# A two-layer decoder trunk on one core: the opening's loads and splits in order of need, MoBA's query projection ahead of the compression MLP, and ends of the attention's values behind the next softmax

## The chip, the cores and the metric

One core of a Trainium2 chip runs the whole program in one launch. The metric is the device time of one execution in microseconds (us), as the median of several runs. TensorE (PE) multiplies, VectorE (DVE) and ScalarE (ACT) do elementwise work, GpSimd (POOL) does a little of it, and SyncE (SP) issues most of the loads. Each engine runs its instructions in the order of the program, and waits on semaphores for the others.

## The reference

Two layers over 256 positions of width 1024, in float32: a SwiGLU block, a mixer of two attentions, a second SwiGLU block, and a norm at the end.

```python
for l in range(DEPTH):
    x = x + 0.5 * _swiglu(_rms(x, ffn1_norm[l]), ffn1_wg[l], ffn1_wu[l], ffn1_wd[l])
    h = _rms(x, mix_norm[l])
    (q_a, g_a, kc, vc, ks_, vs_, kw, vw, q_b, k_b, v_b, gate_a, gate_b) = _split_cols(h @ w_in[l])
    y_a = _nsa(q_a, g_a, kc, vc, ks_, vs_, kw, vw, ...) @ w_branch_nsa[l]
    y_b = _moba(q_b, k_b, v_b) @ w_branch_moba[l]
    merged = jax.nn.sigmoid(gate_a) * y_a + jax.nn.sigmoid(gate_b) * y_b
    x = x + merged @ w_out[l]
    x = x + 0.5 * _swiglu(_rms(x, ffn2_norm[l]), ffn2_wg[l], ffn2_wu[l], ffn2_wd[l])
return _rms(x, final_norm)
```

`_nsa` has 8 query heads in 2 groups. Besides window and selected attention it has a compressed branch: keys and values of 32 positions go through a small MLP (`gelu(flat @ w1) @ w2`), and the queries attend to 15 such summaries. `_moba` is, at this length, causal attention of 8 heads. Queries and keys of both are turned by rotary positions (rope).

## The kernel before, in words

**Numbers as two halves.** A float32 factor is written as `hi + lo`, two tensors that TensorE takes at its fast rate, and a product is three matmuls (`mm3`, lines 147 to 149: hi·hi, lo·hi, hi·lo). So each weight has to be split: ACT copies `raw` to `hi` (line 230, `split_hi`), DVE subtracts `hi` from `raw` to get `lo` (line 237, `split_lo`). Weights come in units of 128 x 2048 values (1 MB); three units of `raw` and four of `hi` and `lo` are held.

**The order of work.** The program is written from the view of TensorE. Each `mm3` is one *tick*. At a tick the program may put in a deferred step (`defer(n, f)`: n ticks later), the split of one more half unit (`split_tick`, every third tick at most), and a step of the *side* work, a generator that holds the attention (`attention`, `attend_all`) and gives TensorE a few transposes or small products every few ticks. So the long projections go on while the attention's chain of softmax and transposes runs through DVE and ACT. All of this is settled when the program is built; on the chip each engine follows its list.

**The mixer.** `ORDER` is the order in which the columns of `w_in` are projected: Q, KV2, G (which holds the keys for compression), QB (MoBA's queries), KB, VB, and four column blocks of the gates GA. `None` stands for `hidden`, the first layer of the compression MLP (`hh`, line 717), whose result ACT copies to `HH` (line 721). Each projection ends in a callback for each of the two row tiles. For queries that is `rope` (lines 528 to 536): three multiplies of DVE that read PSUM, an add, a copy by ACT to the hi half, and a subtraction by DVE for the lo half. The side work goes on with `compress` (`pK`, `X`), `keys_T` (`ksT`, lines 598 to 602), `queries_T` (`pQ`, `qT`, lines 587 and 588), `compress_more` (`hp`, `cp`, `kp`, lines 668 to 706), and then the attention itself: `s1` (scores `s`), `soft` (mask, maximum, exp to `P`), `s2_` (transposes `pt`), `s3` (values `o`), with `finish`, which scales the values on DVE (`aS`, line 616). Side transposes and the projections' PSUM tiles are in few banks: `tr`, `sc`, `a0`, `a1`. A transpose into `tr` waits until the readers of the tile two before have ended; `pQ` so waits for `ksT`'s subtractions on DVE.

**The opening.** `first_piece` computes the first product piece by piece, in eight slices of the first two units. `zeros` are matmuls of zeros that keep TensorE running ahead of it. `gain_columns` transposes the gains of a norm into columns (`pG`, `gcol`). x is transposed (`pT`), multiplied by the gains on DVE (`xg`), copied to hi by ACT and subtracted to lo by DVE (lines 347 to 352). `residual` adds a product to x and defers the transposes of the new x by `wait` ticks.

## Time and profile before

| | us |
|---|---|
| median of 3 runs (lowest, highest) | 1176.99 (1176.88, 1177.0) |
| the profiled execution | 1177.28 |
| its span in the trace | 1175.2 |
| TensorE busy | 1161.5 |
| DVE busy | 730.2 |
| ACT busy | 586.9 |
| POOL busy | 31.2 |

The granted TensorE clock was 0.998 of full speed. A row of the timeline gives start, duration, engine, line, operation, tiles (out<-in), how many instructions in a row it holds, and in brackets the idle time ahead of it with what ended it. A row of the waits gives who waited for whom, the sum, how many times, and the longest. Several instructions of one kind in a row stand in one line, and their duration is then from the first start to the last end. Engines overlap: a step may start while the one before it on the same engine ends, so durations add up to slightly more than the time that passes.

### The profile page before, as it was taken

To read this page: it belongs to the slowest core of one execution; us is meant where nothing else is said; L and a number is where in the kernel's file an instruction comes from. 1 tells how busy PE (TensorE), PEld (TensorE's weight loads), DVE (VectorE), ACT (ScalarE), POOL (GpSimd) and SP (SyncE) were. 2 spreads that over 40 slices of the span, in tenths; PEclk is the share of its full clock that TensorE was granted. 3 is DMA by queue.
4 is the path that set the end of the run, shared out by engine and by line. 5 is a ranking of instruction groups with operands and counts; after the bars stand their busy time and mean duration, and the time that the engine had idled before them with its cause. 6 is when DMAs were issued, how large, how long until landed. Compare 5 with 4: busy or idle time off the path is not lost.

```text
span 1175.2 us, 14436 instructions
## 1 busy us (share of the span) xinstructions
PE 1161.5 (99%) x5689; PEld 974.8 (83%) x5689; DVE 730.2 (62%) x1003; ACT 586.9 (50%) x929; POOL 31.2 (3%) x46
## 2 busy tenths in 40 slices
PE   8999999999999999999999999999999999999997
PEld 6888888988888888888888888889888888888886
DVE  6645546878857665545475455478787577645543
ACT  6444443567465464445364444346665644545332
POOL 2000000000100000000000000000001000000000
PEclk9999999999999999999999999999999999999999
DMA  8755462862444465555546555538434364665540
GB/s 278 258 194 179 144 243 93 208 193 94 143 143 145 143 236 193 185 174 214 180 154 204 187 188 199 174 117 217 144 109 144 117 204 125 238 208 164 180 179 36
DMA packets 103347, 203.53 MB, mean 173 GB/s; under 512 B 4560, under 2 KB 25504, under 8 KB 103280
## 3 DMA queue, kind: packets, MB, share of 16 engines
q1 hardware_dynamic: 102544, 201.84, 52.6%
q8 instruction: 45, 0.74, 0.3%
q10 hardware_dynamic: 432, 0.46, 0.1%
q0 software_dynamic: 304, 0.32, 0.1%
q14 instruction: 22, 0.18, 0.0%
HBM read 201.55 MB, written 1.05 MB: 172 GB/s over the span
## 4 chain that ended last, share of the span: by engine, by line
PE 90%; DVE 5%; ACT 3%; issue 1%; DMA 1%; SPq 0%; POOL 0%; POOLq 0%; DVEq 0%; ACTq 0%
PE pr L147 7%; PE pr L149 7%; PE pr L148 7%; PE dn L149 7%; PE dn L147 7%; PE dn L148 7%; PE u L147 6%; PE u L148 6%; PE u L149 6%; PE g L148 6%; PE g L147 6%; PE g L149 6%; PE pT L383 2%; DVE lo L237 2%; PE o L824 2%; PE gu L147 1%
## 5 line engine op out<-in xcount | busy, mean ns | idle before, releaser
L237 DVE TENSOR_TENSOR lo<-raw,hi 128x1024 fp32r<-128x1024 f32 (+3 forms) x386 | 457.0, 1214 | 209.0 <-ACT hi L230 208.7
L230 ACT CAST hi<-raw 128x1024 fp32r<-128x1024 f32 (+3 forms) x386 | 386.0, 1040 | 269.2 <-PE u L149 106.7
L147 PE MATMUL pr<-hi,hT 128*128 128x512 f32 (+2 forms) x320 | 126.0, 394 | 0.0
L147 PE MATMUL dn<-hi,aTh 128*128 128x512 f32 x318 | 124.6, 392 | 0.0
L147 PE MATMUL u<-hi,hT 128*128 128x512 f32 x320 | 124.6, 389 | 0.0
L149 PE MATMUL u<-hi,hT 128*128 128x512 f32 x320 | 124.5, 389 | 0.0
L148 PE MATMUL u<-lo,hT 128*128 128x512 f32 x320 | 124.5, 389 | 0.0
L149 PE MATMUL dn<-hi,aTl 128*128 128x512 f32 x318 | 123.8, 389 | 0.0
L148 PE MATMUL dn<-lo,aTh 128*128 128x512 f32 x318 | 123.7, 389 | 0.0
L147 PE MATMUL g<-hi,hT 128*128 128x512 f32 x312 | 123.6, 396 | 0.0
L148 PE MATMUL g<-lo,hT 128*128 128x512 f32 x312 | 121.7, 390 | 0.6 <-DVE lo L237 0.5
L149 PE MATMUL pr<-hi,hT 128*128 128x512 f32 (+2 forms) x320 | 122.0, 381 | 0.0
L148 PE MATMUL pr<-lo,hT 128*128 128x512 f32 (+2 forms) x320 | 121.7, 380 | 0.0
L149 PE MATMUL g<-hi,hT 128*128 128x512 f32 x312 | 121.7, 390 | 0.0
L385 DVE TENSOR_TENSOR aTl<-pT,aTh 128x512 fp32r<-128x512 f32 x40 | 25.8, 686 | 72.5 <-ACT aTh L384 72.5
L149 PEld LDWEIGHTS u<-hi,hT 128*128 128x128 f32 x320 | 60.1, 188 | 12.5
L147 PEld LDWEIGHTS u<-hi,hT 128*128 128x128 f32 x320 | 60.1, 188 | 12.5
L148 PEld LDWEIGHTS u<-lo,hT 128*128 128x128 f32 x320 | 60.1, 188 | 12.4
L149 PEld LDWEIGHTS dn<-hi,aTl 128*128 128x128 f32 x318 | 59.7, 188 | 12.4
L148 PEld LDWEIGHTS dn<-lo,aTh 128*128 128x128 f32 x318 | 59.7, 188 | 12.2
L147 PEld LDWEIGHTS dn<-hi,aTh 128*128 128x128 f32 x318 | 59.7, 188 | 12.0
L148 PEld LDWEIGHTS g<-lo,hT 128*128 128x128 f32 x312 | 58.7, 188 | 12.7 <-DVE lo L237 1.4
(221 smaller groups left out, 1584.8 us busy)
## 6 DMA issues: line engine op xcount, KB each, us to landing
raw<-in_ffn_wd SPq DMA_DIRECT2D x44, 1024.0 KB, 5.0
raw<-in_ffn_wu SPq DMA_DIRECT2D x40, 1024.0 KB, 5.1
raw<-in_ffn_wg SPq DMA_DIRECT2D x38, 1024.0 KB, 5.1
raw<-in_w_in SPq DMA_DIRECT2D x32, 1024.0 KB, 5.1
raw<-in_w_out SPq DMA_DIRECT2D x8, 1024.0 KB, 5.0
raw<-in_ffn_wg SPq DMA_DIRECT2D x10, 512.0 KB, 4.0
raw<-in_ffn_wu SPq DMA_DIRECT2D x8, 512.0 KB, 5.0
raw<-in_w_branch_nsa SPq DMA_DIRECT2D x4, 1024.0 KB, 5.1
```

The source lines that it names most:

```text
L147: nc.tensor.matmul(ps, x[0], w[0], start=start, stop=False)
L148: nc.tensor.matmul(ps, x[0], w[1], start=False, stop=False)
L149: nc.tensor.matmul(ps, x[1], w[0], start=False, stop=stop)
L230: nc.scalar.copy(done[i][0][:, a], raws[i][:, a])
L237: nc.vector.tensor_sub(lo[:, a], raws[i][:, a], hi[:, a].bitcast(F32))
L383: nc.tensor.transpose(p[:, k], src[:, 128 * k:128 * k + 128], ident)
L385: defer(1, lambda: nc.vector.tensor_sub(lo, p, hi.bitcast(F32)))
L824: nc.tensor.matmul(O["o"][:, i0 + i], st["pT"][:, i * nk + c], v(h, c, j), start=c == 0, stop=c == nk - 1)
```

## The change: what it does

1. `ORDER`: QB is projected before `hidden`, GA's first block after it. The weights are loaded and split in this order too.
2. `compress_more`: the transposed key `kp` and its split come ahead of the values' product `cp` with its mask `vbd`.
3. `attend_all`: `s3` hands back its end (`finish`, or POOL's sum of the compressed branch), and the end runs behind `soft` of the next pair.
4. `residual`: the ticks until the transposes. In the SwiGLU block, tile 0's second half goes from 4 to 8, tile 1's first half from 5 to 4; in the mixer the first halves go from 17 to 20 and 17.
5. The opening: the first loads are interleaved (x, weight slice, x, slices); the first gain row goes to ACT's queue; the other gains and constants go from POOL's queue to SP's at tick 24, with their columns at ticks 61 to 63; x is scaled straight from PSUM by ACT (hi) and DVE (lo) in slices of 128 columns; the first unit's `hi` is copied by DVE and two of its four `lo` are subtracted by POOL; products are put in as their slices come. The zeros are six and one, not five and three.

```diff
-ORDER = [C_Q, C_KV2, C_G, C_GA, None, C_GA + 512, C_QB, C_KB, C_VB, C_GA + 1024, C_GA + 1536]
+ORDER = [C_Q, C_KV2, C_G, C_QB, None, C_GA, C_GA + 512, C_KB, C_VB, C_GA + 1024, C_GA + 1536]
-WARM = (5, 3)
+WARM = (6, 1)
...
-    nc.sync.dma_start(graw[:, 0], gains[0])
     nc.scalar.dma_start(ident, T["ident"])
+    nc.scalar.dma_start(graw[:, 0], gains[0])
...
-    for what in ((0, 0), (1, 0), 0, 1, 2, 3, (0, 1), (1, 1)):
+    for what in ((0, 0), 0, (1, 0), 1, 2, 3, (0, 1), (1, 1)):
...
-    for j in range(1, len(NORMS)):
-        nc.gpsimd.dma_start(graw[:, j], gains[j])
-    for nm in CONSTS[1:]:
-        nc.gpsimd.dma_start(K[nm], T[nm])
...
+    def load_constants():
+
+        for j in range(1, len(NORMS)):
+            nc.sync.dma_start(graw[:, j], gains[j])
+        for nm in CONSTS[1:]:
+            nc.sync.dma_start(K[nm], T[nm])
...
-                    residual(nxt, t, h, ps[t][h], 4 + t)
+                    residual(nxt, t, h, ps[t][h], 8 if h > t else 4 + t * h)
...
+            yield None
+            kp = bank("tr", "kp", [128, G, 32])
+            nc.tensor.transpose(kp.rearrange("p g c -> p (g c)"), kc2.rearrange("p u d -> p (u d)"), ident[:64, :64])
+            nc.scalar.copy(kbd[:, :, 0], kp[:, :, 0:16])
+            nc.vector.tensor_sub(kbd[:, :, 1], kp[:, :, 0:16], kbd[:, :, 0].bitcast(F32))
             cp = bank("sc", "cp", [128, HD])
             nc.tensor.matmul(cp, hv.rearrange("p h c -> p (h c)"), w2[1], start=True, stop=True)
             vbd[0] = p2.tile([128, NH, HD], F32, name="vbd", tag="vbd", bufs=1)
             nc.vector.tensor_mul(vbd[0], cp[:, None, :].to_broadcast([128, NH, HD]),
                                  K["hmask"][:, :, None].to_broadcast([128, NH, HD]))
-            yield None
-            kp = bank("tr", "kp", [128, G, 32])
...
-                for j in pairs[i - 2]:
-                    j[3]()
+                ends = [j[3]() for j in pairs[i - 2]]
...
                 for j in pairs[i]:
                     j[1]()
+                for end in ends:
+                    if end is not None:
+                        end()
...
-                    lambda t, ps: residual(nxt, t, h, ps, 4 + t if h else 17))
+                    lambda t, ps: residual(nxt, t, h, ps, 4 + t if h else 20 - 3 * t))
...
+        def high(t, h, ks=range(4)):
+
+            for k in ks:
+                f = 4 * h + k
+                nc.scalar.activation(nrm.T[t][0][:, f], p[t][:, k], AF.Copy, scale=nrm.g[:, f:f + 1])
+
+        def low(t, h, ks=range(4)):
+            for k in ks:
+                f = 4 * h + k
+                nc.vector.scalar_tensor_tensor(nrm.T[t][1][:, f], p[t][:, k], nrm.g[:, f:f + 1],
+                                               nrm.T[t][0][:, f].bitcast(F32), op0=OP.mult, op1=OP.subtract)
+
+        def w_high(k):
+            nc.vector.tensor_copy(done[0][0][:, k], raws[0][:, k])
+
+        def w_low(q, k):
+            q.tensor_sub(done[0][1][:, k], raws[0][:, k], done[0][0][:, k].bitcast(F32))
...
-        defer(14 + j, lambda j=j: gain_columns(j))
-    defer(17, more_constants)
+        defer(60 + j, lambda j=j: gain_columns(j))
+    defer(24, load_constants)
+    defer(63, more_constants)
```

**DVE in the mixer.** DVE's list in layer 0 from the weight split ahead of `ksT` to the first small step of the MLP (`hy`), before. `lo<-raw,hi` is a weight's split, `ksT` the keys' second half.

```order
L237 TENSOR_TENSOR lo<-raw,hi 128x1024 x2
L602 TENSOR_TENSOR ksT<-pK_1876,ksT 128x512
L602 TENSOR_TENSOR ksT<-pK_1882,ksT 128x512
L237 TENSOR_TENSOR lo<-raw,hi 128x1024 x5
L674 TENSOR_TENSOR hy<-hx 128x30
```

The same stretch now, up to the last step of the second rope (`rt` and `qb` are QB's rope, one set for each row tile).

```order
L237 TENSOR_TENSOR lo<-raw,hi 128x1024
L531 SCALAR_TENSOR_TENSOR rt_1879<-pr,r,ropeq 128x512
L535 SCALAR_TENSOR_TENSOR rt_1881<-pr,r,ropeq 128x8x32 x2
L537 TENSOR_TENSOR rt_1879<-rt_1879,rt_1881 128x512
L539 TENSOR_TENSOR qb<-rt_1879,qb 128x8x64
L237 TENSOR_TENSOR lo<-raw,hi 128x1024
L605 TENSOR_TENSOR ksT<-pK_1898,ksT 128x512
L605 TENSOR_TENSOR ksT<-pK_1904,ksT 128x512
L237 TENSOR_TENSOR lo<-raw,hi 128x1024
L531 SCALAR_TENSOR_TENSOR rt_1946<-pr,r,ropeq 128x512
L535 SCALAR_TENSOR_TENSOR rt_1948<-pr,r,ropeq 128x8x32 x2
L537 TENSOR_TENSOR rt_1946<-rt_1946,rt_1948 128x512
```

One rope now stands between the two weight splits ahead of `ksT`, the other between `ksT` and the four splits that go ahead of `hy`.

**ACT in the mixer.** ACT's list from the copies of `ksT` to the MLP's `HH`, before. `gt` is the gates' tanh, `qT` NSA's transposed queries.

```order
L601 CAST ksT<-pK_1876 128x512
L601 CAST ksT<-pK_1882 128x512
L588 CAST qT<-pQ 128x512 x2
L920 ACTIVATE gt<-pr,rh 128x512
L230 CAST hi<-raw 128x1024
L588 CAST qT<-pQ 128x512 x2
L230 CAST hi<-raw 128x1024 x2
L721 COPY HH<-hh 128x256
```

And now, where the copies of the ropes (`qb`) stand in place of the tanh.

```order
L538 CAST qb<-rt_1879 128x8x64
L230 CAST hi<-raw 128x1024
L604 CAST ksT<-pK_1898 128x512
L604 CAST ksT<-pK_1904 128x512
L591 CAST qT<-pQ 128x512 x2
L538 CAST qb<-rt_1946 128x8x64
L230 CAST hi<-raw 128x1024
L591 CAST qT<-pQ 128x512 x2
L230 CAST hi<-raw 128x1024 x2
L724 COPY HH<-hh 128x256
```

ACT's second `qb`, which needs DVE's add, stands ahead of the second pair of `qT`, three weight copies and `HH`.

**DVE in the opening.** DVE's list up to the second unit's first split, before (`raw_87` is the first weight unit, `raw_96` the second; `hT_140` and `hT_149` the lo halves of x's two row tiles).

```order
L350 TENSOR_TENSOR xg_155<-pT_150,gcol_118 128x512
L352 TENSOR_TENSOR hT_140<-xg_146,hT_139 128x512
L352 TENSOR_TENSOR hT_149<-xg_155,hT_148 128x512
L237 TENSOR_TENSOR lo_162<-raw_87,hi_161 128x512 x4
L350 TENSOR_TENSOR xg_193<-pT_188,gcol_118 128x512
L350 TENSOR_TENSOR xg_200<-pT_195,gcol_118 128x512
L352 TENSOR_TENSOR hT_140<-xg_193,hT_139 128x512
L237 TENSOR_TENSOR lo_208<-raw_96,hi_207 128x1024
```

And now, from the third of the four copies that ACT did before (`hi_131<-raw_87`); the lo halves of x are `hT_134` and `hT_156`. Ahead of these rows stand two such copies and four steps of 128 columns for the first row tile.

```order
L1002 CAST hi_131<-raw_87 128x512
L998 SCALAR_TENSOR_TENSOR hT_156<-pT_157,gcol_110,hT_155 128x128 x2
L1002 CAST hi_131<-raw_87 128x512
L998 SCALAR_TENSOR_TENSOR hT_156<-pT_157,gcol_110,hT_155 128x128 x2
L1005 TENSOR_TENSOR lo_132<-raw_87,hi_131 128x512 x2
L998 SCALAR_TENSOR_TENSOR hT_134<-pT_181,gcol_110,hT_133 128x128 x4
L998 SCALAR_TENSOR_TENSOR hT_156<-pT_196,gcol_110,hT_155 128x128 x4
L237 TENSOR_TENSOR lo_207<-raw_96,hi_206 128x1024 x2
```

The steps on x of 512 columns, two for each half of a row tile, became sixteen of 128 columns, and the second unit's first split now comes behind all of them. ACT's table load, the first of its list after a transfer in before, stands behind a wait for the gain columns.

## Prediction

> **What bounds the kernel now.** I read the page first, then what TensorE (PE) waits for, then the timelines of the places that the change touches. On the page, the busy line and the chain that ended last:

> ```profile
> PE 1161.5 (99%) x5689; PEld 974.8 (83%) x5689; DVE 730.2 (62%) x1003; ACT 586.9 (50%) x929; POOL 31.2 (3%) x46
> ...
> PE 90%; DVE 5%; ACT 3%; issue 1%; DMA 1%; SPq 0%; POOL 0%; POOLq 0%; DVEq 0%; ACTq 0%
> ```

> TensorE is busy 1161.5 of 1175.2 us, and the change removes no matmul but one of the eight that only warm the engine up. So all that can be won is part of 13.7 us of idle time, and what can be lost is any wait that TensorE does not have yet. The waits of TensorE, longest sum first:

> ```profile
> PE pz L291 <- DVE zero L286: 1.5, 1, 1.5
> PE g L972 <- ACT hi L230: 1.4, 2, 1.2
> PE pt L815 <- ACT P L807: 1.3, 2, 0.7
> PE cp L698 <- issue: 1.2, 2, 0.6
> PE g L148 <- DVE lo L237: 0.5, 1, 0.5
> ```

> The first is the start itself. The second and the last lie in the opening; `pt` and `cp` come once in each of the two mixers. The change aims at these four, 4.4 us together. That is its ceiling, up to short gaps that this view leaves out.

> **The opening.** Four rows of before, from the timelines of ACT, DVE and PE:

> ```profile
> 1.19 1.28 ACT L351 ACT_TABLE_LOAD   x1 [1.19 <-PEq L1033]
> ```
> ```profile
> 4.21 0.17 DVE L304 COPY gcol<-pG 128x16 f32<-128x16 f32 x1 [2.81 <-PE pG L303]
> ...
> 14.67 1.22 DVE L237 TENSOR_TENSOR lo<-raw,hi 128x1024 fp32r<-128x1024 f32 x1 [0.26 <-ACT hi L230]
> ```
> ```profile
> 15.94 0.50 PE L148 MATMUL g<-lo,hT 128*128 128x512 f32 x1 [0.47 <-DVE lo L237]
> ```

> Earlier loads and smaller pieces let the first true product start sooner: the 1.4 us behind `hi` shrink, since a slice of raw weight is now copied as soon as it lands. But the opening is over only when the first product of the second weight unit has its `lo` (15.94 here, with DVE done at 15.89), and DVE decides that in the new order too. The table load is now behind the gain columns, so it starts near 4.4 + 0.3 (one more warming matmul ahead of them) and ends near 6.0, not at 2.47. The four scaled copies of x go there, then DVE's part. Prices for the small operations, from the same kinds on PSUM in the mixer (ACT's row first, then three that show DVE and the bank it frees):

> ```profile
> 215.40 0.36 ACT L902 ACTIVATE vv<-pr,r 128x128 f32<-128x128 f32 x1
> ```
> ```profile
> 216.05 0.35 DVE L528 SCALAR_TENSOR_TENSOR rt<-pr,r,c_rope 128x128 f32<-128x128 f32 x1
> 216.32 0.47 DVE L532 SCALAR_TENSOR_TENSOR rt<-pr,r,c_rope 128x64 f32<-128x64 f32 x2
> ```
> ```profile
> 217.16 0.34 PE L147 MATMUL pr<-hi,hT 128*128 128x408 f32 x1
> ```

> A 128-wide step costs DVE 0.27 (216.05 to 216.32), an ACT one about the same. From 6.0 four ACT copies take it to 7.1; then DVE has sixteen such steps (4.3), three of the four copies of raw weight and two subtractions of 512 columns, at about half of the 1.22 of the 1024-column row each (1.8 and 1.2), in all to 14.4 if it never idles. It does idle, for each next half of x has to be transposed and copied by ACT first: an estimate of 1.2 for three such hand-overs of about 0.4 (ACT's row and its semaphore). That is 15.6, and with the 1.22 of the first big `lo` 16.8, against 15.89: about 0.9 late. Two transposes of gain columns (moved to ticks 61 and 62) cost the same there. Less the warming matmul and the small gap that the earlier split of the next unit closes, I take +0.5. The lower bound is -1.4, the whole wait behind `hi`, if DVE never idles and the weight copies are quick. The upper is +2, below. No row shows a copy of fp32 from SBUF by DVE: bounds 0.2 and 0.69 each. [...]

> The nine constants' transfers go from POOL's queue to SP's, behind the first eight weight units and ahead of the next ones. At 0.4 to 0.5 of issue each they hold the next load by some 4 us; no row of the waits above names a DMA as TensorE's releaser, three raw units and four split ones stand ahead, and I cost it at nothing (bound +1).

> Two subtractions move to POOL. How the two engines get on, from the timelines of POOL and DVE at 305 us, and DVE alone at 244:

> ```profile
> 22.09 1.24 POOL L361 TENSOR_TENSOR r<-v,magic 128x1 f32<-128x1 f32 x2 [15.53 <-DVE v L357]
> ...
> 309.73 3.52 POOL L774 TENSOR_TENSOR A<-A,aC 128x512 f32<-128x512 f32 x2 [2.62 <-DVE aC L616]
> ```
> ```profile
> 244.61 3.50 DVE L237 TENSOR_TENSOR lo<-raw,hi 128x1024 fp32r<-128x1024 f32 x3 [0.69 <-ACT hi L230]
> ...
> 310.11 5.37 DVE L237 TENSOR_TENSOR lo<-raw,hi 128x1024 fp32r<-128x1024 f32 x3
> ```

> Three subtractions took 5.37 beside POOL and 3.50 without it: 1.9 for two POOL steps. In the opening most DVE steps read PSUM, so only a weight copy can meet a POOL step, once or twice: 0 to 1, taken at 0 within the +0.5. [...]

> **The mixer, MoBA's queries ahead of the MLP.** This is the term that decides. Before, DVE, ACT and PE ahead of and behind the hidden products:

> ```profile
> 234.39 2.35 DVE L237 TENSOR_TENSOR lo<-raw,hi 128x1024 fp32r<-128x1024 f32 x2
> 237.00 1.29 DVE L602 TENSOR_TENSOR ksT<-pK,ksT 128x512 fp32r<-128x512 f32 x2 [0.25 <-ACT ksT L601]
> ...
> 242.69 1.22 DVE L237 TENSOR_TENSOR lo<-raw,hi 128x1024 fp32r<-128x1024 f32 x1 [3.27 <-ACT hi L230]
> ```
> ```profile
> 240.05 1.08 ACT L588 CAST qT<-pQ 128x512 fp32r<-128x512 f32 x2 [2.60 <-PE pQ L587]
> ...
> 243.48 2.04 ACT L230 CAST hi<-raw 128x1024 fp32r<-128x1024 f32 x2
> 245.38 0.42 ACT L721 COPY HH<-hh 128x256 f32<-128x256 f32 x1
> ```
> ```profile
> 239.41 1.03 PE L587 MATMUL pQ<-c_ident,qa 128*128 128x128 f32 x8
> ...
> 245.85 0.41 PE L668 MATMUL hp<-c_sel,HH 128*128 128x32 f32 x2
> ...
> 250.60 0.33 PE L689 MATMUL cp<-w,hk 128*64 128x64 f32 x2
> ...
> 254.21 1.22 PE L796 MATMUL s<-ksT,qT 128*128 128x256 f32 x8
> ```

> What is put in there is the rope of QB, once per row tile, as it stands in before inside NSA's attention:

> ```profile
> 273.21 0.74 DVE L528 SCALAR_TENSOR_TENSOR rt<-pr,r,ropeq 128x512 f32<-128x512 f32 x1
> 273.88 0.86 DVE L532 SCALAR_TENSOR_TENSOR rt<-pr,r,ropeq 128x256 f32<-128x256 f32 x2
> ...
> 276.77 1.22 DVE L237 TENSOR_TENSOR lo<-raw,hi 128x1024 fp32r<-128x1024 f32 x1
> ```
> ```profile
> 275.50 0.62 ACT L535 CAST qb<-rt 128x512 fp32r<-128x512 f32 x1 [1.28 <-DVE rt L534]
> ```

> One rope holds DVE 3.56 (273.21 to 276.77), a handover to ACT in it; ACT's copy starts 2.29 after its first step. The new order puts the first between the two subtractions at 234.39, ahead of `ksT`. These `ksT` subtractions free the two banks that `pQ` needs, and pQ comes behind the same number of products as before. So `ksT` starts at 237.00 + 3.56 - 0.25 = 240.3, the first bank is free 0.65 later, at 240.95, and pQ starts 1.55 late. ksT's second ends at 241.6, one weight subtraction follows to 242.7, then the second rope; ACT's copy for it starts at 242.7 + 2.29 = 245.0. Behind it on ACT stand one weight copy (half of 2.04), two `qT` (1.08), two weight copies (2.04) and HH (0.42): 245.0 + 0.62 + 1.02 + 1.08 + 2.04 + 0.42 is 250.2, less some 0.1 of overlap at each of four joints 249.8. HH was done at 245.8, and `hp` on TensorE, which takes it, came right behind: 249.8 against 245.85, **3.9 late**. pQ's 1.55 and a wait for the first `lo` of the next unit lie within this.

> What could make it less: DVE's 3.27 of idle time at 239.4. But that idle comes behind `ksT`, and the rope is put ahead of it; it can only shorten what follows. Bounds: 2.4, if ACT is held by half of its queue alone, and 4.9, if the hand-overs cost more.

> **The key and value columns behind it.** `kp` is now ahead of the values' `cp`. DVE's end of kc and the value mask in before:

> ```profile
> 252.94 0.28 DVE L696 TENSOR_TENSOR kc<-ct,ct 64x128 f32<-64x128 f32 x1
> 253.15 0.68 DVE L700 TENSOR_TENSOR vbd<-cp,c_hmask 128x512 f32<-128x512 f32 x1
> ```

> kc is done 2.62 after cp (250.60 to 253.22), and `s` starts 3.61 after cp. The 0.6 wait of the second cp goes. But the mask now stands on DVE behind a weight subtraction (1.14) and the small step on kbd (0.1), and the scores' bank is free when it ends: 2.62 + 1.14 + 0.1 + 0.68 = 4.5, **0.9 later**, the cp wait already counted. Bounds -0.6 and +1.3; I take 0.8.

> **Ends behind the softmax, and no rope beside it.**

> ```profile
> 281.08 0.89 PE L815 MATMUL pt<-c_ident,P 128*128 128x128 f32 x4 [0.67 <-ACT P L807]
> ```

> DVE reaches this softmax late because the rope and the end of the values stand ahead of it. Both are gone from there, so the 0.67 goes with the shorter gap behind it: **-1.0** (bounds -0.6 and -1.2). The bank that an end frees comes up to two softmax steps later, and the next `o` is far enough behind: nothing, bound +0.5.

> **Later transposes.** The second half of row tile 0 is transposed eight ticks after its sum, not four. DVE then takes Q's rope later, and its margin at project G is 216.79 (216.32 + 0.47, bank freed) to 217.16. A multiply and a subtraction of 0.7 each that come late break it: 0 to 1.0, I take +0.4.

> **Sum.** Per layer 3.9 + 0.8 - 1.0 + 0.4 = +4.1, twice 8.2, opening 0.5: +8.7. The profiled execution took 1177.28, its span 1175.2 and 2.1 around it; the sum gives 1186.0 there. The median of the runs is 0.3 lower, so **1185.7**. With the bounds of its terms the case reaches from 1181 to 1190.

> **The rivals.**
> - *Slower, by POOL.* The first subtraction on POOL can start near 5.0 (gain columns at 4.4, one weight copy) and be done near 6.8, at half of 3.52. The product that needs it comes near 13: 15.94 less the wait of 0.47, one product and eight more at some 0.23 apart. If something holds POOL for longer than these 6 us, TensorE waits for the rest, and DVE's next two subtractions meet it as at 310.11: 1 to 2 above the forecast's opening, 1187. Against it: the first two POOL steps of before, at 22.09, took 1.24 together, with no gap. [...]
> - *No change.* pQ's 1.55 stays, and ACT has caught up by HH, so nothing of the rest: 1.55 + 0.2 - 1.0 - 0.6 per layer is about 0.2, with an opening of 0: 1177.3.
> - *Faster.* The rope costs nothing where it is put, since DVE's 3.27 and 0.69 of idle time (242.69, 244.61) hold both. Then the waits removed are all there is: per layer -1.0 - 0.6, twice, and -1.0 in the opening: 1172.8. It decides if pQ starts less than about 0.5 late. For it: 4 us of DVE idle before HH. Against it: the idle is behind `ksT`, and the two ropes take 7.1.

> **Chances.** Forecast 0.66, POOL 0.07, no change 0.10, faster 0.17. Slower 0.73, same 0.10, faster 0.17, where same is within 0.2%, or 2.4 us, about what a measurement of this kernel can tell from no change. The forecast's own range is 1181 to 1190. The range 1175 to 1189.5 adds the no-change case and leaves out most of the faster one and the top.

> **What would show it.** Right: TensorE's waits in both mixers name `pQ` on DVE (1.5 or so), `hp` on ACT's HH (over 1), `s` on DVE; `pt` and the second `cp` are gone; in the opening the first L148 starts near 16.9. Wrong: pQ within 0.5 of its product ahead, or HH's copy close behind `hh`. If the opening's L148 starts at 15 or earlier, DVE was quicker there than I count, and the opening term is a gain.

## The result, and the profile after

The changed kernel took 1190.93 us (median of four runs, 1187.64 to 1191.47) against 1176.99; the ratio is 1.0106, with a 95% interval of 1.0094 to 1.0119. So it is 12.5 us slower by the ratio and 13.9 by the medians. The direction and the cause in the mixers were forecast; the size, 8.7, was too small. The median lies 0.9 above the forecast's own range (1181 to 1190) and 1.4 above the other (1175 to 1189.5); the ratio times 1176.99 gives 1189.5, inside the first and at the edge of the second. The profiled execution took 1191.47, its span 1189.7, 14.5 more than before.

The busy times on the page of the changed kernel:

```profile
PE 1169.6 (98%) x5688; PEld 979.7 (82%) x5688; DVE 732.2 (62%) x1013; ACT 587.5 (49%) x937; POOL 34.3 (3%) x39
```

TensorE's busy time rose by 8.1 us, though it has one matmul fewer. That is the first thing to see: waits do not count as busy, so something made the matmuls themselves longer. The waits of TensorE in the changed kernel:

```profile
PE pQ L590 <- DVE ksT L605: 3.0, 2, 1.5
PE hp L671 <- ACT HH L724: 2.3, 2, 1.1
PE g L148 <- DVE lo L237: 1.8, 1, 1.8
...
PE pr L147 <- DVE rt L535: 1.2, 2, 0.6
PE pr L148 <- DVE lo L237: 1.2, 2, 0.6
...
PE s L801 <- DVE vbd L708: 0.5, 2, 0.3
```

`pt` and the second `cp` are gone, as forecast. Once in each layer there are now waits of `pQ`, of `hp`, of the first `lo` of GA, of `s`, and of the projection of G (`pr` for DVE's `rt`). The next table shows where the time went, by the start of the same product in both timelines. The last column is run e8 (below), in which TensorE is kept busy in its longest waits:

| place (TensorE) | before | after | late | late in e8 |
|---|---|---|---|---|
| first product of u, layer 0 | 22.32 | 26.57 | 4.25 | 0.40 |
| first product of dn | 135.75 | 140.63 | 4.88 | 1.02 |
| first `hh`, layer 0 | 240.21 | 247.88 | 7.67 | 3.82 |
| first `hp` | 245.85 | 255.51 | 9.66 | 5.81 |
| second `hp` | 248.24 | 259.47 | 11.23 | 5.80 |
| a product of the scores `s`, ahead of the old `pt` wait | 266.70 | 277.83 | 11.13 | 6.24 |
| one behind the old `pt` wait | 289.15 | 299.00 | 9.85 | 4.96 |
| just behind layer 0 (a product of u in layer 1's first block) | 605.51 | 615.23 | 9.72 | 4.91 |
| layer 1, second block (a product of dn) | 1108.49 | 1123.09 | 14.60 | 8.72 |

The mixer's chain in layer 0 of the changed kernel, as DVE, ACT and PE show it (rows that stand for those of before at 237.00, 245.38, 239.41 and 245.85):

```profile
244.38 0.69 DVE L539 TENSOR_TENSOR qb<-rt,qb 128x512 fp32r<-128x512 f32 x1 [0.69 <-ACT qb L538]
244.99 1.22 DVE L237 TENSOR_TENSOR lo<-raw,hi 128x1024 fp32r<-128x1024 f32 x1
246.13 1.28 DVE L605 TENSOR_TENSOR ksT<-pK,ksT 128x512 fp32r<-128x512 f32 x2
```
```profile
250.75 0.62 ACT L538 CAST qb<-rt 128x512 fp32r<-128x512 f32 x1 [2.00 <-DVE rt L537]
...
255.07 0.38 ACT L724 COPY HH<-hh 128x256 f32<-128x256 f32 x1
```
```profile
246.87 1.25 PE L590 MATMUL pQ<-c_ident,qa 128*128 128x128 f32 x8 [1.50 <-DVE ksT L605]
...
255.51 0.41 PE L671 MATMUL hp<-c_sel,HH 128*128 128x32 f32 x2 [1.14 <-ACT HH L724]
```

The rope and a weight split end at 246.2, then `ksT` frees the bank and pQ starts 1.5 after TensorE was ready; the second rope's copy on ACT starts at 250.75, and HH comes behind one weight copy, two `qT` and two more weight copies. HH is done at 255.45. Less the 5.8 by which TensorE is late ahead of `pQ`'s wait (4.9 from the opening, 0.9 at the projection of G) this is 249.7 in the times of before, where the forecast had 249.8.

What made the matmuls longer shows in the windows view. Its columns are the busy times of PE, PEld, DVE, ACT and POOL with the number of instructions, then PEclk (the granted TensorE clock as a share), the share of the DMA engines, and GB/s:

```profile
17.13:20.55 3.42, 1.57 (x7) 1.02 (x6) 3.27 (x6) 3.42 (x6) 0.00 (x0) 1.00 0.24 91
20.55:23.96 3.41, 3.41 (x10) 2.63 (x9) 2.84 (x7) 3.35 (x10) 0.54 (x1) 0.50 0.58 183
```
```profile
245.83:249.24 3.41, 2.37 (x19) 2.20 (x20) 3.41 (x6) 1.61 (x3) 0.00 (x0) 1.00 0.02 5
...
252.65:256.06 3.41, 1.68 (x8) 0.89 (x7) 2.72 (x3) 3.41 (x6) 0.00 (x0) 1.00 0.06 22
256.06:259.48 3.42, 3.42 (x10) 2.63 (x9) 2.55 (x7) 1.57 (x4) 0.00 (x0) 0.50 0.84 281
```

The granted clock is cut in steps of 3.41 us that all lie on one grid. Behind a step in which TensorE was busy for 1.57 or 1.68 of 3.41, the next runs at half speed (a *fall* of the clock, below); behind one of 2.37 it does not. The clock falls at 20.55, at 256.06 and at 839.74 in layer 1, which is 2, 71 and 242 steps behind its first full speed at 13.72, and each time behind the waits that the change brought. In such a step matmuls of 512 columns come every 0.43 and not every 0.23, and about 1.6 us are lost: between the two `hp` of the table the changed kernel falls back by 1.57, where e8 does not. Before, the clock did not fall between 6.2 us and 1170. The emptiest step there was the first:

```profile
6.23:9.64 3.41, 2.03 (x8) 1.08 (x8) 1.52 (x3) 2.50 (x5) 0.34 (x4) 1.00 1.03 362
```

The clock has a second part in the opening. TensorE's first products before, and in the changed kernel below them:

```profile
8.10 0.51 PE L972 MATMUL g<-hi,hT 128*128 128x512 f32 x1 [1.17 <-ACT hi L230]
8.82 2.79 PE L972 MATMUL g<-hi,hT 128*128 128x512 f32 x11 [0.21 <-ACT hi L230]
```

```profile
6.82 0.80 PE L976 MATMUL g<-hi,hT 128*128 128x512 f32 x1 [0.54 <-ACT hT L993]
...
9.28 4.19 PE L976 MATMUL g<-hi,hT 128*128 128x512 f32 x9
...
19.59 0.50 PE L148 MATMUL g<-lo,hT 128*128 128x512 f32 x1 [1.85 <-DVE lo L237]
```

The first product does start earlier, at 6.82 against 8.10. But nine products take 4.19 us where eleven took 2.79 before, since TensorE did not come to full speed until 13.7 (6.2 before); up to then its products come every 0.43. The transposes behind them, and with them DVE's part, move along, and the first `lo` product is at 19.59, not 15.94 as before or near 16.9 as forecast. In e8, where TensorE is at full speed from 6.7, it is at 17.37.

### The profile page after: what moved, and what is told of

It is laid out like the page before. It is cut to its first block, busy times and chain, and to the rows that moved or that the text cites. A ratio compares the mean times of both kernels' runs of the same rounds, so it can differ in the third digit from the quotient of the medians.

```text
span 1189.7 us, 14437 instructions
## 1 busy us (share of the span) xinstructions
PE 1169.6 (98%) x5688; PEld 979.7 (82%) x5688; DVE 732.2 (62%) x1013; ACT 587.5 (49%) x937; POOL 34.3 (3%) x39
## 4 chain that ended last, share of the span: by engine, by line
PE 89%; DVE 6%; ACT 3%; issue 1%; DMA 1%; POOL 0%; SPq 0%; POOLq 0%; ACTq 0%; DVEq 0%
PE dn L149 7%; PE dn L148 7%; PE dn L147 7%; PE pr L147 6%; PE pr L149 6%; PE pr L148 6%; PE u L147 6%; PE u L148 6%; PE u L149 6%; PE g L149 6%; PE g L148 6%; PE g L147 6%; PE o L829 3%; PE pT L386 2%; DVE lo L237 2%; PE s L801 2%
## 5 line engine op out<-in xcount | busy, mean ns | idle before, releaser
L237 DVE TENSOR_TENSOR lo<-raw,hi 128x1024 fp32r<-128x1024 f32 (+1 forms) x382 | 455.6, 1223 | 201.9 <-ACT hi L230 201.4
L230 ACT CAST hi<-raw 128x1024 fp32r<-128x1024 f32 (+1 forms) x382 | 383.1, 1044 | 272.2 <-PE u L149 110.4
L147 PE MATMUL pr<-hi,hT 128*128 128x512 f32 (+2 forms) x320 | 127.3, 398 | 1.2 <-DVE rt L535 1.2
L147 PE MATMUL u<-hi,hT 128*128 128x512 f32 x320 | 124.7, 390 | 0.0
L148 PE MATMUL u<-lo,hT 128*128 128x512 f32 x320 | 124.5, 389 | 0.0
L148 PE MATMUL pr<-lo,hT 128*128 128x512 f32 (+2 forms) x320 | 123.2, 385 | 1.2 <-DVE lo L237 1.2
L147 PE MATMUL dn<-hi,aTh 128*128 128x512 f32 x318 | 124.4, 391 | 0.0
L147 PE MATMUL g<-hi,hT 128*128 128x512 f32 x312 | 124.0, 398 | 0.0
L148 PE MATMUL g<-lo,hT 128*128 128x512 f32 x312 | 122.1, 391 | 1.8 <-DVE lo L237 1.8
L148 PE MATMUL dn<-lo,aTh 128*128 128x512 f32 x318 | 123.7, 389 | 0.0
L149 PE MATMUL pr<-hi,hT 128*128 128x512 f32 (+2 forms) x320 | 123.4, 386 | 0.0
L148 PEld LDWEIGHTS g<-lo,hT 128*128 128x128 f32 x312 | 59.1, 189 | 13.9 <-DVE lo L237 2.3
L149 PEld LDWEIGHTS u<-hi,hT 128*128 128x128 f32 x320 | 60.1, 188 | 12.5
L147 PEld LDWEIGHTS u<-hi,hT 128*128 128x128 f32 x320 | 60.1, 188 | 12.5
L148 PEld LDWEIGHTS u<-lo,hT 128*128 128x128 f32 x320 | 60.1, 188 | 12.4
L147 PEld LDWEIGHTS pr<-hi,hT 128*128 128x128 f32 x320 | 60.7, 190 | 11.5 <-ACT hi L230 1.8
L148 PEld LDWEIGHTS pr<-lo,hT 128*128 128x128 f32 x320 | 60.8, 190 | 11.1 <-DVE lo L237 1.8
```

Of the source, the lines that this page charges most:

```text
L147: nc.tensor.matmul(ps, x[0], w[0], start=start, stop=False)
L148: nc.tensor.matmul(ps, x[0], w[1], start=False, stop=False)
L149: nc.tensor.matmul(ps, x[1], w[0], start=False, stop=stop)
L230: nc.scalar.copy(done[i][0][:, a], raws[i][:, a])
L237: nc.vector.tensor_sub(lo[:, a], raws[i][:, a], hi[:, a].bitcast(F32))
```

## The experiments

Two theories were tried. **The forecast's:** the engines' lists are worked in order, and the ropes put ahead of `ksT` and HH make TensorE wait. **The clock:** on top of that, waits that fill about half a step of 3.41 us cost another 1.6 us behind them, and in the opening they delay full speed. The rivals: that the order of the projections is not what costs, that the waits are all there is, or that a bank is the cause. Times are medians; the ratio and its interval are to runs of the kernel before on the same chip. The runs were made on three chips: e1 to e4, e5 to e8, and e9 to e12.

| run | median us | ratio to before (95%) |
|---|---|---|
| the changed kernel | 1190.93 | 1.0106 (1.0094 to 1.0119) |
| e1 order only | 1183.32 | 1.0045 (1.0033 to 1.0058) |
| e2 old order | 1178.81 | 1.0011 (1.0002 to 1.0019) |
| e3 old opening | 1187.60 | 1.0080 (1.0066 to 1.0094) |
| e4 ends only | 1174.95 | 0.9980 (0.9971 to 0.9989) |
| e5 fill in the opening | 1187.61 | 1.0083 (1.0069 to 1.0097) |
| e6 zeros in the first gaps | 1186.77 | 1.0079 (1.0065 to 1.0093) |
| e7 fill in the mixers | 1185.63 | 1.0080 (1.0066 to 1.0094) |
| e8 all three fills | 1185.82 | 1.0069 (1.0056 to 1.0082) |
| e9 ends, and zeros in the first gaps | 1174.77 | 0.9973 (0.9964 to 0.9983) |
| e10 residual only | 1179.49 | 1.0013 (1.0004 to 1.0022) |
| e11 kp only | 1177.26 | 0.9999 (0.9990 to 1.0008) |
| e12 keys in another bank | 1190.18 | 1.0099 (1.0084 to 1.0115) |

### e1: the new ORDER alone

```diff
-ORDER = [C_Q, C_KV2, C_G, C_GA, None, C_GA + 512, C_QB, C_KB, C_VB, C_GA + 1024, C_GA + 1536]
+ORDER = [C_Q, C_KV2, C_G, C_QB, None, C_GA, C_GA + 512, C_KB, C_VB, C_GA + 1024, C_GA + 1536]
```

> The kernel before with the new ORDER alone. Theory (in-order lists, and a TensorE clock that falls to half for 3.4 us behind a stretch with about 2 us of idle time): pQ waits 1.5 on DVE, hp 1.1 to 1.4 on ACT's HH, the first lo 0.6, in both layers, the pt wait of 0.7 goes, the second cp wait stays; and the granted clock falls once in each mixer, for 1.6 to 1.7. Per layer 3.9 - 1.2 + 1.6, twice: about 1185.5. Rival A (the waits without the clock): 1182.4. Rival B (the order of the projections is not what costs, but the opening): within 2 of before.

Its waits, and the steps of its grid that hold the waits ahead of `hp` in layer 0 and part of those in layer 1:

```profile
PE pQ L587 <- DVE ksT L602: 3.0, 2, 1.5
PE hp L668 <- ACT HH L721: 2.3, 2, 1.1
```
```profile
246.38:249.79 3.41, 1.69 (x10) 0.94 (x8) 2.53 (x3) 3.41 (x7) 0.00 (x0) 1.00 0.28 105
```
```profile
819.82:823.23 3.41, 1.99 (x9) 1.31 (x7) 2.72 (x5) 2.54 (x4) 0.00 (x0) 1.00 0.75 278
```

The waits are those of the changed kernel to the tenth. In layer 0 `hp` is 3.87 late (my sum: 3.9). The clock fell there, behind the step with 1.69 busy; it did not fall in layer 1, where the same waits lie across the joints of the grid and the emptiest step had 1.99. So layer 0 ends 3.5 late and layer 1 adds 2.5. The five times lie at 1183.4 with a clock of 0.997 and at 1182.4 with 0.999. Both theories are half met: the waits alone are rival A's 1182.4, and the clock adds 1 on some executions only, less than I gave it.

The `pt` wait is gone in this run too, as expected, though the end of the values still stands ahead of the softmax. The row that waited 0.67 before starts without a wait, and the products behind it win back 1.3 in each layer:

```profile
285.07 0.61 PE L815 MATMUL pt<-c_ident,P 128*128 128x128 f32 x4
```

### e2: the changed kernel with the old ORDER

```diff
-ORDER = [C_Q, C_KV2, C_G, C_QB, None, C_GA, C_GA + 512, C_KB, C_VB, C_GA + 1024, C_GA + 1536]
+ORDER = [C_Q, C_KV2, C_G, C_GA, None, C_GA + 512, C_QB, C_KB, C_VB, C_GA + 1024, C_GA + 1536]
```

> The changed kernel with the old ORDER. Theory: no pQ, hp or lo waits in the mixers and no fall of the clock there; what stays is the opening (4.9 late after the gain columns) and the later transposes (0.9 per layer), less the pt waits that the ends behind the softmax take away (1.0 each): about 1181. Rival B (the opening holds nearly all): 1188 or more.

```profile
PE g L148 <- DVE lo L237: 1.8, 1, 1.8
...
PE s L801 <- DVE vbd L708: 1.3, 2, 0.7
PE pr L147 <- DVE rt L535: 1.1, 2, 0.6
```

It is 1178.81, 12 below the changed kernel and 0.1% above before: rival B falls, the order is what costs most. In its profiled execution the opening is 4.88 late, as in the changed kernel, and each mixer then adds 0.9 at project G and 0.4 at the scores and gives 1.3 back: nothing. That execution took 1181.57; the eleven lie between 1177.76 and 1181.57, which is 0 to 4 above the median of before on this chip. Since the mixers come out even, I put this down to the opening; only one of the eleven was profiled.

### e3: the changed kernel with the opening of before

The loads, zeros, splits and constants of before, with ORDER, `residual`, `compress_more` and `attend_all` of the changed kernel.

> The changed kernel with the opening of before (loads, splits, zeros, constants), all mixer changes kept. Theory: the opening costs 4 to 5 in the changed kernel, so 1186 to 1187, with the mixer waits as in the changed kernel and two falls of the clock. Rival (the opening costs the 0.5 of the forecast, and the rest of the 13.9 is in the mixers): 1190.

1187.60, with the waits in both mixers, but a fall of the clock in layer 1 alone (835.22) and not in both. It is some 3 below the changed kernel, by the medians or the ratios, whose intervals just touch. That is the opening's share, less than the 4 to 5 expected. In this profile the opening of before was itself 1.68 late at the first u, with a fall at 9.19.

### e4: the ends behind the softmax, alone

```diff
-                for j in pairs[i - 2]:
-                    j[3]()
+                ends = [j[3]() for j in pairs[i - 2]]
...
+                for end in ends:
+                    if end is not None:
+                        end()
```

> The kernel before with the ends of the values behind the softmax alone (attend_all and s3). Theory: the softmax on DVE comes 1.3 earlier, which takes the pt wait away in both layers though the rope is still there: 1.0 to 1.2 per layer, 1174.6 to 1175.0. Rival (the rope alone holds the softmax up, and the ends only move the wait to the next values): 1177.

DVE's timeline, where the softmax steps (L804, L806) now stand ahead of the end (`cf`, `aS`):

```profile
279.31 1.22 DVE L237 TENSOR_TENSOR lo<-raw,hi 128x1024 fp32r<-128x1024 f32 x1
280.45 0.42 DVE L804 TENSOR_TENSOR s<-s,c_causal 128x256 f32<-128x256 f32 x1
280.91 0.69 DVE L806 TENSOR_REDUCE m<-s 128x2 f32<-128x512 f32 x1
```

The `pt` wait is in none of its waits, and the same products lie 1.28 earlier in layer 0 and 1.33 in layer 1, with the rope still in its place. So moving the end is enough, and the rival falls. But moving the rope is enough too (e1), for the same 1.3 per layer. They are two ways to win one wait, and not two gains: the new ORDER takes the wait away also without the ends. Alone, without the new ORDER, this part of the change is worth 0.2%.

### e5 to e8: useless matmuls in the waits

e5 adds seven zeros ahead of the first mm3, e6 more zeros in the first gaps, e7 matmuls into a bank of their own ahead of pQ (seven) and hp (five), e8 all of it. Every part of the computation stays.

```diff
+        zeros(7)                          # e5, at the end of first_piece
-WARM = (6, 1)
+WARM = (6, 3)                             # e6
+        zeros(3)                          # e6, between the first two products
+            idle(7)                       # e7, ahead of queries_T(qa, qaT)
+                if j == 0:
+                    idle(5)               # e7, ahead of the first hp
...
+        def idle(n):
+            pz = bank("sc", "pi", [128, 512])
+            h = nrm.T[0][0]
+            for i in range(n):
+                nc.tensor.matmul(pz, h[:, 0], h[:, 0:4].rearrange("p a b -> p (a b)"), start=i == 0, stop=i == n - 1)
```

> The changed kernel with seven useless matmuls of zeros more at the end of first_piece, where TensorE waits 1.85 for the first lo of the second unit; they leave out nothing. Theory of the clock: the zeros take 1.6 of that wait, the stretch counts as busy, and the fall to half behind it (20.5 to 24.0) goes: 1.7 faster than the changed kernel, 1189.2. Rival (the clock does not look at idle time, or the slow stretch has another cause): the same time or up to 0.3 more, since seven matmuls are added.

> The changed kernel with five zeros more in the first gaps: (6, 3) instead of (6, 1), and three between the first two products. Theory of the clock: full speed comes near 7 to 10 and not at 13.7, which saves up to 13 of the 19 slow products at 0.2 each, 2 to 2.7, of which the later wait for lo (DVE sets it, from the transposes that TensorE does) takes back a part: 1 to 2.5 faster than the changed kernel, 1188.4 to 1189.9. Rival (DVE's chain alone sets the end of the opening): the same time.

> The changed kernel with useless matmuls in both mixers: seven of 512 columns ahead of pQ, five ahead of the first hp, into a bank of their own. Theory of the clock: the waits for DVE and ACT stay as long, but TensorE is busy in them, and the falls of the clock (256.1 and 839.7) go: 3.2 faster than the changed kernel, 1187.7, with 24 matmuls more. Rival (waits alone): the same time or more.

> The three fillings together. Theory: the gains add up to what the waits alone cost, 1183 to 1185, with a granted clock of 1 from about 10 us to the end. Rival: 1190.

The steps that were too empty are fuller now, in e5 (the first `lo`) and in e7 (ahead of `hp`):

```profile
18.26:21.67 3.41, 3.34 (x15) 2.77 (x16) 3.41 (x5) 3.38 (x8) 0.00 (x0) 1.00 0.27 54
```
```profile
252.34:255.76 3.42, 2.83 (x14) 1.88 (x14) 2.73 (x3) 3.42 (x6) 0.00 (x0) 1.00 0.17 64
```

All four are faster than the changed kernel though they have more matmuls: by 3.3, 4.2, 5.3 and 5.1 at the medians. They may have run on another chip than it did; by the ratios to before it is 0.23, 0.27, 0.26 and 0.37%, where the intervals of e5 and e7 reach that of the changed kernel's (1.0094), e6's ends just below it and e8's (up to 1.0082) lies clear of it. A fill takes away the falls where it is, and no others: e5's profile still falls at 253.78 in layer 0, and e6's at 18.68 and in both mixers. In e7's profile no step in a mixer is slow, and in e8's none at all from 6.7 to 1180.9, 2.9 us ahead of the end (mean clock 0.999). What the rival has in its favour is only that e7's profiled execution, whose opening stays slow, took 1189.35. By the medians the first three won more than expected (1.7, up to 2.5, and 3.2), and e8 less: it stayed above its 1183 to 1185. In e5 it was not the added zeros alone: ahead of them its profile was at full speed from 4.6 to 8.0 and again from 11.4, and that of the changed kernel only from 13.7. So the fills do not add up by their medians: e8 is no faster than e7, whose five times lie at 1185.6 or at 1189.3. But e8's own five lie within 0.3, and the others' within 1 to 3.8. In e6 and e7 the times go with the mean clock (e7: 1189.3 at 0.997, 1185.6 at 0.998 and 0.999; e6: 1189.22 at 0.994, 1187.63 at 0.995, 1186.6 to 1186.8 at 0.996); in e5 they do not (1186.75 and 1187.53 at 0.996, 1187.69 and 1187.73 at 0.998).

The waits that are left in e8:

```profile
PE s L809 <- DVE vbd L710: 1.3, 2, 0.7
PE pr L148 <- DVE lo L237: 1.2, 2, 0.6
PE pr L147 <- DVE rt L535: 1.2, 2, 0.6
```

e8 is thus the changed kernel without the falls of the clock: it is 8.7 late near the end, and the sum of the forecast was 8.7. Its last column in the table above splits this as opening 1.0 and 3.9 and 3.8 for the mixers.

### e9: the ends, and zeros in the first gaps of before

```diff
-WARM = (5, 3)
+WARM = (5, 5)
-        some(0, 0, 0, (0, 1))
+        some(0, 0, 0, (0,))
+        zeros(1)
+        some(0, 0, 0, (1,))
```

with e4's edit.

> The kernel before with the ends behind the softmax, and three zeros more in the opening's first gaps: (5, 5) for (5, 3), and one between the first two products. Theory: the ends give 1.3 per layer, and the zeros keep the first gap from counting as idle, so that the clock falls in the opening in no execution: 1174.7 with a spread under 1. Rival (the spread of before, 1176.6 to 1179.7, has another cause than where the clock's stretches lie): the same median as with the ends alone and the same spread of 3.

PE's first products here, and in e4 below it:

```profile
6.10 2.08 PE L291 MATMUL pz<-zero 128*128 128x512 f32 x5
8.29 0.50 PE L973 MATMUL g<-hi,hT 128*128 128x512 f32 x1
8.63 0.39 PE L291 MATMUL pz<-zero 128*128 128x512 f32 x1
8.86 2.81 PE L973 MATMUL g<-hi,hT 128*128 128x512 f32 x11
```
```profile
8.15 0.50 PE L973 MATMUL g<-hi,hT 128*128 128x512 f32 x1 [1.13 <-ACT hi L230]
10.36 4.14 PE L973 MATMUL g<-hi,hT 128*128 128x512 f32 x11 [1.70 <-ACT hi L230]
```

This beats both kernels: 1174.77, 0.27% below before, and nine times within 0.8 (1174.30 to 1175.06), where those of before on the same chip spread over 3.3, and e4's eleven, on another chip, over 3.1. By the ratios e9 and e4 cannot be told apart. In e4's profile the second wait for `hi` was 1.70, the step behind it ran at half speed, and eleven products took 4.14, not 2.81. The zeros closed the gap here. In e4's profile ACT also had to wait longer for the second slice of raw weight; how much of the scatter is the loads and how much the clock, these runs do not part.

### e10, e11: residual's ticks alone, kp ahead of cp alone

```diff
-                    residual(nxt, t, h, ps[t][h], 4 + t)
+                    residual(nxt, t, h, ps[t][h], 8 if h > t else 4 + t * h)
-                    lambda t, ps: residual(nxt, t, h, ps, 4 + t if h else 17))
+                    lambda t, ps: residual(nxt, t, h, ps, 4 + t if h else 20 - 3 * t))
```

> The kernel before with the new waits of residual alone. Theory: one wait of 0.6 (0.9 by start times) at project G in each layer, nothing else: 1.9 slower, 1179.2. Rival (it is the opening's lateness that breaks the margin there): the same time as before.

e11 moves the five lines of kp, and the `yield` ahead of them, between kc2 and the second cp, as in the change.

> The kernel before with kp ahead of the values' cp alone. Theory: the 0.6 wait of cp goes, s waits 0.7 for the mask on DVE in its place; 0.4 late at the scores, part of it given back at the pt wait that follows: within 1 of before in both directions. Rival (the forecast's 0.8 per layer): 1.6 slower.

```profile
PE pr L147 <- DVE rt L532: 1.1, 2, 0.6
```
```profile
PE s L796 <- DVE vbd L705: 1.3, 2, 0.7
PE pt L815 <- ACT P L807: 0.4, 2, 0.2
```

e10 shows the wait at project G, 0.6 by the view and 0.8 to 0.9 by starts in each layer, without the new opening: its rival falls. It is 1.4 later at the end of its profile; 1.9 was expected. e11 trades the cp wait for one of `s`, is 0.4 late there, and gets it back at `pt`: no change that can be measured.

### e12: NSA's keys in another bank

```diff
-        def keys_T(src, pairs, hi, lo):
+        def keys_T(src, pairs, hi, lo, tag="tr"):
-                p = bank("tr", "pK2", [128, 2, S])
+                p = bank(tag, "pK2", [128, 2, S])
```

with "sc" passed for NSA's keys. The wait of pQ for the bank is taken away by the bank.

> The changed kernel with NSA's transposed keys in the sc bank, so that pQ no longer waits for their subtractions on DVE. Theory (the queues of DVE and ACT are late as a whole, and HH is what ends last): pQ's 1.5 goes, the same time appears at the next products (a wait of 1.5 for the hi of GA's first block and 0.9 for its lo) and hp starts as late as before: the changed kernel's time within 1. Rival (the bank is the cause): 3 faster, and with the falls of the clock gone 6 faster.

```profile
251.37 0.50 PE L147 MATMUL pr<-hi,hT 128*128 128x512 f32 x1 [1.44 <-ACT hi L230]
...
252.63 0.50 PE L148 MATMUL pr<-lo,hT 128*128 128x512 f32 x1 [0.76 <-DVE lo L237]
...
254.50 0.51 PE L671 MATMUL hp<-c_sel,HH 128*128 128x32 f32 x2 [1.15 <-ACT HH L724]
```

pQ no longer waits, and the same 1.5 stands one stage later, at the first weights of GA. `hp` is 3.87 later against `hh` than before, as much as `pQ` and `hp` together with the old bank, and the time is that of the changed kernel. The bank was where the lateness showed, not where it came from.

## Why the prediction was right, and where it fell short

1. **QB's rope ahead of the MLP** (forecast 3.9 per layer at `hp`): shown. 3.87 in e1 and in e12, and 1.87 + 1.98 in e8 (ahead of `hh`, and from there to `hp`). The reason, that the two ropes on DVE and their copies on ACT stand ahead of `ksT` and HH, holds against the bank (e12) and the rest of the change (e1, e2). The rival that the rope fits into DVE's 3.27 of idle time fell: `pQ` waited 1.5 and HH came late, since that idle time stands behind `ksT`.
2. **The keys' and values' columns** (0.8): mis-sized, 0.4 (e8, e11). The mask does stand behind a weight split on DVE, but only the second half of the first scores waits for it: in the changed kernel four of the eight matmuls of `s` start at 264.84 without a wait, and the other four at 265.82. I had all of `s` start behind the mask.
3. **The ends, and no rope beside them** (-1.0): -1.28 to -1.33 (e4, e1), a little beyond my bound of -1.2. I named both as the reason; each is enough alone, so inside the whole change the moved ends had nothing left to win at `pt`.
4. **The later transposes** (0.4): 0.8 to 0.9 (e10), the upper part of my bounds (0 to 1.0).
5. **The four together**: 4.1 per layer forecast, 3.9 and 3.8 in e8. The errors of 2, 3 and 4 nearly cancel, which is luck.
6. **The opening** (0.5): this step failed. At full clock it is 1.0 (e8). In the changed kernel it is 4.9 in the profiled execution and some 3 by the medians (e3), above my upper bound of +2. I took TensorE's pace in the new opening to be that of before, took off the removed zero as a gain, and asked only what DVE does. The row that I should have weighed is that of the zeros, which I counted as work to be saved: full speed came at 6.2 with eight (before), at 13.7 with seven (the changed kernel) and at 6.7 with twelve in the first gaps (e8); but in e5, with the same seven there, it came at 4.6, was lost from 8.0 to 11.4, and came back. My prices on DVE were near: three of its copies of raw weight took 0.42 where I had counted 0.6, and one beside POOL took 1.20. The 0.6 and its bounds of 0.2 and 0.69 were estimates, for no row of before shows such a copy. The constants cost nothing, as counted: their nine issues on SP took 0.33 to 0.58 each, held the next load from 30.87 to 36.49, and TensorE has no wait from 27 to 100.
7. **The clock in the mixers**: not in the sum at all, and without a reason given. I priced each wait at its length; two falls of some 1.5 to 1.6 come on top in the profiled execution.
8. **POOL as a rival**: fell. Its two subtractions started at 5.43 and 8.60 and took 1.27 each (rows below).

So the waits cost what the forecast had for the whole, 8.7, and the 4 to 6 above it (0.37% by the ratios of e8 and the changed kernel, 5.8 us between the profiles) are the clock, in the opening and behind the waits. That the two 8.7 agree to the tenth is luck: in e8 the mixers took 0.5 less than forecast, and the opening 0.5 more.

## What to carry to other kernels

Where TensorE is busy 99% of the time, price a step that is moved by what stands behind it on the lists of DVE and ACT, up to the next thing that TensorE takes from either; a free bank (e12) or idle time elsewhere on the list changed nothing here. Price a wait of TensorE at its length, and ask beside it how empty the 3.4 us around it become: in the changed kernel the waits of 0.6 and 1.1, which lie close together, brought a fall of the clock, and the one of 1.5 alone did not. Useless matmuls in a wait that cannot be removed cost nothing here and kept the clock up (e5 to e8: 3.3 to 5.3 faster at the medians than the changed kernel; mean clock 0.999 in e8's profile and 0.994 in the changed kernel's). Of a change with several parts, try the parts: of the four tried alone here (e1, e4, e10, e11) one was a gain, and the new ORDER already holds that gain within its loss.

## What the runs showed of the hardware

**The granted clock is set by steps of 3.41 us on a fixed grid.** Over the profiles of before, of the changed kernel and of the twelve runs, I took TensorE's busy time in every step of each profile's grid between the first full speed and 1160 us, as the windows view counts it. The 19 steps that are followed by one at half speed had 1.09 to 1.89 us busy; the fullest of them is in e5, ahead of 253.78. All other steps, followed by full speed, were fuller; the emptiest of them had 1.91 (in e1):

```profile
250.37:253.78 3.41, 1.89 (x8) 1.33 (x9) 2.72 (x4) 3.23 (x6) 0.00 (x0) 1.00 0.09 14
```
```profile
239.55:242.96 3.41, 1.91 (x16) 1.70 (x16) 3.41 (x5) 2.10 (x4) 0.00 (x0) 1.00 0.21 76
```

**A DVE copy beside POOL took longer.** From the timelines of POOL and DVE in the changed kernel's opening:

```profile
5.43 1.27 POOL L1005 TENSOR_TENSOR lo<-raw,hi 128x512 fp32r<-128x512 f32 x1 [4.38 <-DVE hi L1002]
8.60 1.27 POOL L1005 TENSOR_TENSOR lo<-raw,hi 128x512 fp32r<-128x512 f32 x1 [1.90 <-DVE hi L1002]
```
```profile
4.94 0.42 DVE L1002 CAST hi<-raw 128x512 fp32r<-128x512 f32 x1
...
8.95 1.20 DVE L1002 CAST hi<-raw 128x512 fp32r<-128x512 f32 x1
```

A copy of 512 columns takes 0.42 alone, quicker than a subtraction of that size (two took 1.28), and 1.20 when it starts while POOL runs: it ended at 10.15, 0.28 behind POOL's end at 9.87. The same copy took 1.20 or 1.21 in e2, e6, e8 and e12. What makes it longer, no run here shows. The forecast had 0 to 1 for such a meeting, and it cost DVE 0.8.

The steps of DVE that read PSUM and met a POOL step here kept their time. Two of 128 columns took 0.60 from 8.43 on, beside POOL's step at 8.60, and 0.60 from 11.70 on without POOL. Before, the first step of a rope took 0.74 beside POOL, as it did without it at 273.21:

```profile
306.37 0.74 POOL L852 TENSOR_TENSOR A<-aS 128x256 f32<-128x256 f32 x1 [14.44 <-DVE aS L616]
```
```profile
306.20 0.74 DVE L528 SCALAR_TENSOR_TENSOR rt<-pr,r,c_rope 128x512 f32<-128x512 f32 x1
```

**Products of halves are the faster ones.** At full clock they come every 0.23 with 512 columns; the four matmuls of the float32 product `co`, 512 columns wide too, start 0.43 apart (before):

```profile
306.92 1.88 PE L773 MATMUL co<-vbd,cpT 128*128 128x512 f32 x4
```
